# A hybrid decoder trunk on one core: evictions and gate additions issued with high priority

## The chip, the core and the metric

The kernel runs on one core of a Trainium2 chip. A core has a matrix engine (TensorE, PE in the profile, with its weight loads listed as PEld), three engines for element-wise work (VectorE or DVE, ScalarE or ACT, GpSimd or POOL) and SyncE (SP), which here only issues DMAs. Each engine has a queue of its own and works it off in order; engines wait for one another through semaphores. TensorE writes its results into PSUM, eight banks of 128 x 512 float32; another engine has to read a bank out ("evict" it) before it can be filled again.

The metric is device time in microseconds (us). The kernel before takes 806.76 us, the median of three runs (806.67 to 806.95).

## The reference, cut to what matters

Two residual layers over 256 tokens of width 1024. Each layer normalises the stream, multiplies it by one wide input matrix, feeds three causal mixers (a state-space scan, "SSD"; sliding-window attention with sinks, "SWA"; forgetting attention, "FOX"), projects each, weights the three by sigmoid gates with a bias, adds them, and applies an output projection:

```python
for layer in range(DEPTH):
    h = rms_norm(x, norm_w[layer])
    proj = jnp.einsum('bsd,de->bse', h, w_in[layer])
    (a_xbc, a_z, a_dt, b_q, b_k, b_v, b_z,
     c_q, c_k, c_v, c_f, c_z, gates) = jnp.split(proj, split_at, axis=-1)
    y_a = mamba2_branch(a_xbc, a_z, a_dt, ...)
    y_b = sliding_window_branch(b_q, b_k, b_v, b_z, ...)
    y_c = forgetting_attention_branch(c_q, c_k, c_v, c_f, c_z, ...)
    ys = jnp.stack([y_a, y_b, y_c], axis=2)
    branch = jnp.einsum('bsiw,iwd->bsid', ys, w_proj[layer])
    g = jax.nn.sigmoid(gates.reshape(b, s, N_BRANCH, d) + gate_bias[layer])
    merged = jnp.sum(g * branch, axis=2)
    x = x + jnp.einsum('bsd,de->bse', merged, w_out[layer])
return rms_norm(x, final_norm_w)
```

Everything is float32.

## The kernel before

**Products in three parts.** A float32 matrix is split into a high part, rounded to the format in which TensorE multiplies at full pace, and a low part, the remainder. A product is high x high + low x high + high x low. The splitting is work of its own: ScalarE copies the high part (line 290), VectorE subtracts it (line 291). Weights arrive as "raw" tiles of 128 x 1024 through SyncE's DMAs (line 360), six buffers deep, and are split into tiles `hi` and `lo`, six buffers each, up to four parts ahead of their use.

**Units.** The input matrix is worked off in units. A unit with *tokens on partitions* (`tok`) leaves a bank of 128 tokens x up to 512 columns. A unit with *channels on partitions* (`both_sums`) leaves 128 channels x 256 tokens, and it does so in one bank with two halves: the left half holds two of the three products, the right half the third. An eviction therefore has to add the halves, and there are two ways:

- `chan_sum` (lines 473 to 479): ScalarE copies the right half into the output (478), then VectorE adds the left half to it (479).
- `dma_sum` (lines 481 to 489): ScalarE copies both halves (486, 487), and a DMA issued by GpSimd adds one to the other in memory (488).

The keys, queries and gate paths of SWA, the convolution inputs of SSD and the first four key and query units of FOX use `dma_sum`; the gate paths of SSD and FOX and the other FOX units use `chan_sum`. Units write into three banks named `mm`; all other products (scores, transposes, scans) mostly use five banks named `mx`.

**Gates.** `u_gate` (line 1097 on) multiplies a 512-column unit of the gates, adds the bias from a tile that a DMA has spread over the partitions (VectorE, line 1106, or line 1108 in the first units, where the normalisation is still to be applied), and takes a tanh of half of it on ScalarE (1109). The merge (`merge`, from line 1134) multiplies the projected branch by the gate and adds it up; for the FOX branch it is issued with high priority. So are the output's operations in `out_end` (1205 on) and the sums of `u_proj_normed` (1017, 1019).

**What sets the order.** The order of TensorE's instructions is written out by hand: operations run in a fixed list, and the attention and scan steps are slipped in between by a small planner (`launch`, `pump`) that counts TensorE time and holds each step back for a fixed delay, so that its inputs are ready when TensorE comes to it. The other engines' order isn't written out after the first 13 us: a scheduler walks through the program and, whenever an engine is free in its model of time, takes the ready instruction with the lowest priority number. The number is the place in the program text, so earlier text goes first. Inside `with tc.high_priority():` it is that of the program's beginning, so such an instruction goes ahead of all other ready ones. On the chip the queues that come out of this are worked off strictly in order.

**Work hung behind evictions.** `finish(ins)` issues the deferred work of earlier units (convolution taps, rotations, gates' SiLU; list `ends_later`) and orders it behind the given instruction on that instruction's engine. `after_evictions(3, f)` puts f behind the third eviction from there, by when the accumulating DMA has landed.

**The window heads' softmax.** `attn_quad` handles four heads at once. For SWA, VectorE takes the row maxima (615, 623, 624), ScalarE the exponentials (610), VectorE the reciprocal sums and the product with them (638, 639); then TensorE transposes the probabilities (`mx<-ident,pp`, line 113).

Of the kernel before, what the change touches and what calls it, by code (L numbers as in the profile page):

```python
# [13 lines left out]
AF = mybir.ActivationFunctionType  # L14
ALU = mybir.AluOpType

P = 128
S = 256
# [32 lines left out]
def hybrid_trunk(  # L51
# [17 lines left out]
    def T(tag, shape, dtype=F32, bufs=None):  # L69
        count[0] += 1  # L70
        return sb.tile(shape, dtype, tag=tag, name=f"{tag}_{count[0]}",
                       bufs=bufs if bufs is not None else BUFS.get(tag, 1))
# [5 lines left out]
    def pmm():  # L78
        return PS("mm", 3)

    def pmx():
        return PS("mx", 5)

    act = nc.scalar.activation
    stt = nc.vector.scalar_tensor_tensor
    tt = nc.vector.tensor_tensor
# [63 lines left out]
    def pump(budget=BUDGET):  # L150
        t0 = clock["t"]
        half = False
        while True:
            over = clock["t"] - t0 >= budget
            if over and not half:
                return
            for m in sorted(waiting, key=lambda m: (m[5] and m[2] != 0, m[0], m[1])):
                if ready(m) and (m[5] if over else not early(m)):
                    half = m[5]
                    enter(m)  # L160
                    break
            else:
                return
# [112 lines left out]
    def ordered(ap):  # L276

        return ap.rearrange("p (i a) -> p a i", a=2)

    def halves(ap):  # L280

        return ap.rearrange("p (a i) -> p a i", a=2)
# [142 lines left out]
    for l in range(L):  # L425
        y = Layer()
# [46 lines left out]
    def chan_sum(y, w, c, out):  # L473


        p = pmm()
        both_sums(y, w, c, p)
        finish(act(halves(out), ordered(p[:, S:2 * S]), AF.Copy))
        tt(halves(out), ordered(p[:, 0:S]), halves(out), op=ALU.add)

    def dma_sum(y, w, c, out):

        p = pmm()
        both_sums(y, w, c, p)
        lo = T("L1", [P, S])
        act(halves(lo), ordered(p[:, S:2 * S]), AF.Copy)  # L486
        last = act(halves(out), ordered(p[:, 0:S]), AF.Copy)  # L487
        nc.gpsimd.dma_start(out, lo, accum_op=ALU.add)  # L488
        finish(last)

# [4 lines left out]
    def both_sums(y, w, c, p):  # L495
        for k in range(NK):
            if k > 0:
                mm(p[:, 0:S], w.lo(k)[:, c:c + P], tokens_in_turn(y.hTh, k), start=False, stop=False)
            mm(p, w.hi(k)[:, c:c + P], y.hT[:, k, :, :, :].rearrange("p a h i -> p (h i) a"),
               start=(k == 0), stop=(k == NK - 1))  # L500
            if k == 0:
                mm(p[:, 0:S], w.lo(k)[:, c:c + P], tokens_in_turn(y.hTh, k), start=False, stop=False)
            if w.last and (k + 1) % w.kper == 0:
                release(w, k // w.kper + 1)

    def tok(ah, al, w, t, turn=True, mid=None):


        n = w.n
        p = pmm()  # L510
        b = in_turn if turn else lambda ap: ap
        if mid is None and n > 300:
            mid = pump
        dense(p[:, 0:n], lambda k: ah[:, t, k, :], lambda k: al[:, t, k, :], lambda k: b(w.hi(k)),
              lambda k: b(w.lo(k)), w, mid=mid)
        return ordered(p[:, 0:n]) if turn else p[:, 0:n]
# [22 lines left out]
    def rotated(y, done):  # L539

        held = {}

        def u(half):
            def f(w):
                p = T("L1", [P, S])
                dma_sum(y, w, half * P, p)

                def turned():
                    for i in (half, 1 - half):
                        m = held[half, i] = T("L1", [P, S])  # L550
                        tt(m, p, cs[:, i, :], op=ALU.mult)  # L551
                    if half == 1:
                        done(held)
                after_evictions(3, turned)
                pump()
            return f
        return u(0), u(1)
# [256 lines left out]
    def u_conv(y, u, c):  # L814
        def f(w):
            if u == 8:
                y.bcT = T("L8", [P, 8, S])
            if u == 0:
                y.xs = T("L8", [P, 8, S])
            dst = y.xs[:, u, :] if u < 8 else y.bcT[:, u - 8, :]  # L820
            x_ = T("L1", [P, S])
            dma_sum(y, w, c, x_)

            def taps():
                a = T("L1", [P, S])
                act(a, x_, AF.Identity, scale=y.vec[:, 48 + u:49 + u], bias=y.vec[:, 64 + u:65 + u])  # L826
                for j in (2, 1, 0):
                    s = 3 - j
                    stt(a[:, s:S], x_[:, 0:S - s], y.vec[:, 16 * j + u:16 * j + u + 1], a[:, s:S],  # L829
                        op0=ALU.mult, op1=ALU.add)  # L830
                ends_later.append(lambda: end(a))

            def end(a):
                th = T("L1", [P, S])
                act(th, a, AF.Tanh)
                stt(dst, th, 1.0, a, op0=ALU.add, op1=ALU.mult)
                if u < 8 and u % 2 == 1:
                    launch(0, ssd_group(y, u // 2), D_G0)
            after_evictions(3, taps)
            pump()  # L840
        return f
# [4 lines left out]
    def finish(out):  # L846

        with tc.issue_after(out.ins):
            for _ in range(len(ends_later)):
                ends_later.pop(0)()  # L850
# [80 lines left out]
    def u_z(y, br, u, c):  # L931
        def f(w):
# [12 lines left out]
            if br == 1:  # L945
                dma_sum(y, w, c, o)
                after_evictions(3, gated)
                pump()
                return
            chan_sum(y, w, c, o)  # L950

            def normed():
# [92 lines left out]
    def u_ck(y, j, c):  # L1045
        def f(w):
            y.ckT[j] = T("qt", [P, 2, S])
            (dma_sum if j < EARLY else chan_sum)(y, w, c, y.ckT[j][:, 0, :])
            if j % 2 == 0:
                launch(2, fox_quad(y, j), D_FOX)  # L1050
            pump()
        return f

    def u_cq(y, j, c):
        def f(w):
            (dma_sum if j < EARLY else chan_sum)(y, w, c, y.ckT[j][:, 1, :])
            y.cqdone[j] = clock["t"] + (D_ADD if j < EARLY else 0.0)
            pump()
        return f
# [37 lines left out]
    def u_gate(y, br, c, t):  # L1097

        def f(w):
            if t == 0:  # L1100
                y.gb = T("L2", [P, 512])
                nc.scalar.dma_start(y.gb, gate_bias[y.l, br:br + 1, c:c + 512].to_broadcast([P, 512]))
            p = tok(y.hTh, y.hTl, w, t)
            g = T("L2", [P, 512])
            if y.rn is None:
                tt(halves(g), p, halves(y.gb), op=ALU.add)  # L1106
            else:
                stt(halves(g), p, y.rn[:, t:t + 1], halves(y.gb), op0=ALU.mult, op1=ALU.add)
            finish(act(g, g, AF.Tanh, scale=0.5))  # L1109
            y.gate[br, c, t] = g  # L1110
            pump()
        return f
# [312 lines left out]
    with tc.manual_schedule(engines={ENG.PE, ENG.DVE, ENG.Activation, ENG.Pool}):  # L1425
# [11 lines left out]
        p = pmx()  # L1437
# [93 lines left out]
        for i in range(2):  # L1531
# [6 lines left out]
                                op=ALU.add)  # L1538
# [53 lines left out]
```

## Time and profile before

| what | value |
|---|---|
| median of three runs | 806.76 us (806.67 to 806.95) |
| span of the profiled execution, first to last instruction | 805.1 us |
| what the median has beyond that span | 1.66 us |
| TensorE busy | 796.5 us (99%), mean granted clock 0.998 |
| VectorE busy | 684.2 us (85%) |
| ScalarE busy | 533.8 us (66%) |
| GpSimd busy | 167.5 us (21%) |

The profiled execution's own time outside of the profiler is not recorded separately; its span of 805.1 us is what the durations add up to, and 1.66 us lie around it in the median run.

How to read the lines: a group's line gives source line, engine, operation, output<-inputs by their tile tags (`L` stands for the general tiles L1, L2, L4, L8 and L16, `mm` and `mx` for the banks), shapes, the count, then busy time and mean ns, then the idle time of the engine just before these instructions and what ended it. A timeline line gives start, duration, engine, line, operation and count. A stretch's line gives start:end, its length, then the busy time of TensorE, weight loads, VectorE, ScalarE and GpSimd, the granted clock, the DMA share and GB/s. Matmuls overlap: one is recorded as longer than the distance to the next.

### The profile page before, as it was taken

How to read it: one execution, taken by the hardware profiler on the slowest of the kernel's cores; microseconds unless marked ns; L12 is line 12 of the kernel's file. 1: busy time of each engine (PE TensorE's matmuls, PEld its weight loads, DVE VectorE, ACT ScalarE, POOL GpSimd, SP SyncE). 2: the span in 40 equal slices, each digit the busy share in tenths (PEclk: the TensorE clock that was granted, in tenths of full speed). 3: DMA queues.
4: the chain of work that ended last, by engine and by line, in shares of the span. 5: the costliest groups of instructions: out<-in, count | busy, mean ns of one | idle time of the engine just before them, and what ended most of it. 6: DMA issues, size and time to landing. Idle time of an engine off the chain costs nothing.

```text
span 805.1 us, 14840 instructions
## 1 busy us (share of the span) xinstructions
PE 796.5 (99%) x5160; PEld 711.6 (88%) x5160; DVE 684.2 (85%) x1416; ACT 533.8 (66%) x1146; POOL 167.5 (21%) x236
## 2 busy tenths in 40 slices
PE   9999999999999999999999999999999999999996
PEld 8998988888998988888998899888889989888896
DVE  6878999997998997795785799999889999969865
ACT  7776768875775885543665678687657768755452
POOL 3166213140210100033001741122311220002000
PEclk9999999999999999999999999999999999999999
DMA  9997987797765565686678987679976546576632
GB/s 316 280 259 172 253 219 200 219 290 220 198 184 167 174 187 170 219 253 205 217 251 257 239 210 217 157 217 287 285 211 196 183 143 202 156 248 210 209 106 78
DMA packets 138827, 170.43 MB, mean 212 GB/s; under 512 B 9353, under 2 KB 106465, under 8 KB 138753
## 3 DMA queue, kind: packets, MB, share of 16 engines
q1 hardware_dynamic: 114960, 140.53, 55.5%
q0 software_dynamic: 13328, 13.29, 10.3%
q10 hardware_dynamic: 10464, 15.67, 6.7%
q8 instruction: 41, 0.67, 0.3%
q14 instruction: 34, 0.27, 0.1%
HBM read 154.71 MB, written 2.16 MB: 195 GB/s over the span
## 4 chain that ended last, share of the span: by engine, by line
PE 91%; issue 3%; DMA 2%; POOL 2%; DVE 1%; ACT 1%; POOLq 0%; DVEq 0%
PE mm L109 78%; PE mx L109 9%; PE mx L113 4%; DMA L<-L 1%; DMA hb<-in_sinks_dram 1%; POOL L L488 1%; DMA L<-in_x_dram 0%; DVE L L551 0%; ACT pp L610 0%; POOL L L285 0%; POOL L L562 0%; DVE lo L291 0%; POOL sm L224 0%; POOL L L571 0%; POOL L L572 0%
## 5 line engine op out<-in xcount | busy, mean ns | idle before, releaser
L109 PE MATMUL mm<-L,hi 128*128 128x512 f32 x1056 | 354.7, 387 | 0.5 <-ACT L L487 0.3
L291 DVE TENSOR_TENSOR lo<-raw,hi 128x1024 fp32r<-128x1024 f32 (+1 forms) x276 | 313.3, 1154 | 40.9 <-ACT hi L290 36.1
L109 PE MATMUL mm<-hi,L 128*128 128x512 f32 (+2 forms) x1168 | 303.1, 349 | 0.1
L290 ACT ACTIVATE hi<-raw 128x1024 fp32r<-128x1024 f32 (+1 forms) x276 | 265.6, 982 | 50.6 <-PE mm L109 30.0
L109 PE MATMUL mm<-L,lo 128*128 128x256 f32 x1056 | 266.6, 273 | 0.0
L109 PEld LDWEIGHTS mm<-hi,L 128*128 128x128 f32 x1168 | 205.8, 190 | 23.2 <-issue 1.5
L109 PEld LDWEIGHTS mm<-L,hi 128*128 128x128 f32 x1056 | 195.1, 190 | 27.4 <-issue 3.0
L109 PEld LDWEIGHTS mm<-L,lo 128*128 128x128 f32 x1056 | 202.1, 191 | 5.3
L109 PE MATMUL mm<-lo,L 128*128 128x512 f32 (+2 forms) x584 | 201.5, 347 | 0.0
L109 PEld LDWEIGHTS mm<-lo,L 128*128 128x128 f32 x584 | 110.2, 190 | 10.7
L488 POOL DMA_DIRECT2D L<-L x68 | 60.7, 915 | 192.5 <-ACT L L487 155.2
L1074 POOL TENSOR_SCALAR_AFFINE_SELECT bias<-bias 128x128 f32<-128x128 f32 x64 | 30.8, 513 | 82.7 <-DMA bias<-cumd 82.7
L829 DVE SCALAR_TENSOR_TENSOR L<-L,vec,L 128x255 f32<-128x255 f32 (+2 forms) x96 | 46.2, 481 | 1.9 <-ACT L L826 0.4
L486 ACT ACTIVATE L<-mm 128x256 f32<-128x256 f32 x84 | 31.9, 380 | 20.0 <-PE mm L109 14.0
L652 ACT ACTIVATE pp<-pp,nm 128x128 f32<-128x128 f32 x64 | 28.2, 443 | 22.8 <-DVE nm L646 22.8
L1109 ACT ACTIVATE L<-L 128x512 f32<-128x512 f32 x24 | 15.1, 631 | 34.5 <-DVE L L1106 30.8
L610 ACT ACTIVATE pp<-pp,nm 128x128 f32<-128x128 f32 x32 | 12.6, 394 | 24.9 <-DVE nm L615 24.1
L488 POOL DMA_DIRECT2D qt<-L x16 | 14.2, 925 | 71.4 <-ACT qt L487 64.6
L1142 POOL TENSOR_TENSOR L<-L,L 128x512 f32<-128x512 f32 x8 | 12.0, 1494 | 74.0 <-DVE L L1141 74.0
L487 ACT ACTIVATE L<-mm 128x256 f32<-128x256 f32 x68 | 26.2, 386 | 1.5 <-DMA L<-L 1.5
L1106 DVE TENSOR_TENSOR L<-mm,L 128x512 f32<-128x512 f32 x22 | 15.1, 687 | 11.2 <-PE mm L109 11.2
L551 DVE TENSOR_TENSOR L<-L,cs 128x256 f32<-128x256 f32 x40 | 20.0, 536 | 4.6 <-DMA L<-L 4.6
(213 smaller groups left out, 913.7 us busy)
## 6 DMA issues: line engine op xcount, KB each, us to landing
raw<-in_w_in_dram SPq DMA_DIRECT2D x191, 512.0 KB, 5.1
raw<-in_w_proj_dram SPq DMA_DIRECT2D x48, 512.0 KB, 6.0
L<-L POOLq DMA_DIRECT2D x72, 128.0 KB, 5.4
raw<-in_w_out_dram SPq DMA_DIRECT2D x16, 512.0 KB, 5.9
bias<-cumd ACTq DMA_DIRECT2D x16, 256.0 KB, 3.4
L<-cumd ACTq DMA_DIRECT2D x8, 512.0 KB, 5.4
L<-in_gate_bias_dram ACTq DMA_DIRECT2D x12, 256.0 KB, 5.4
qt<-L POOLq DMA_DIRECT2D x16, 128.0 KB, 6.0
```

The source lines that it names most:

```text
L109: nc.tensor.matmul(o, a, b, **kw)
L113: nc.tensor.transpose(o, a, i)
L290: keep(act)(hi, src, AF.Copy)
L291: keep(tt)(lo, src, hi.bitcast(F32), op=ALU.subtract)
L486: act(halves(lo), ordered(p[:, S:2 * S]), AF.Copy)
L487: last = act(halves(out), ordered(p[:, 0:S]), AF.Copy)
L488: nc.gpsimd.dma_start(out, lo, accum_op=ALU.add)
L551: tt(m, p, cs[:, i, :], op=ALU.mult)
L652: act(pp[:, i, sl], pp[:, i, sl], AF.Exp, scale=-1.0, bias=nm[:, e:e + 1], accum_out=sums[:, e:e + 1])
L829: stt(a[:, s:S], x_[:, 0:S - s], y.vec[:, 16 * j + u:16 * j + u + 1], a[:, s:S], op0=ALU.mult, op1=ALU.add)
L1074: nc.gpsimd.affine_select(out=bias[:, i, dst], in_=bias[:, i, src], compare_op=ALU.is_ge, fill=NEG, base=0, pattern=[[-1, P]], channel_mul ...
L1106: tt(halves(g), p, halves(y.gb), op=ALU.add)
```

## The change

In three places, reads of a bank are wrapped in `tc.high_priority()`: both steps of `chan_sum`, both copies of `dma_sum`, and the addition of the gates' bias in `u_gate`. In `chan_sum` the call of `finish` moves behind the addition, so deferred work that was written between the copy and the addition is now written behind both; it is still ordered behind the copy. The accumulating DMA of `dma_sum` and the gates' tanh keep their priority. No instruction is added or taken away.

```diff
         p = pmm()
         both_sums(y, w, c, p)
-        finish(act(halves(out), ordered(p[:, S:2 * S]), AF.Copy))
-        tt(halves(out), ordered(p[:, 0:S]), halves(out), op=ALU.add)
+        with tc.high_priority():
+            half = act(halves(out), ordered(p[:, S:2 * S]), AF.Copy)
+            tt(halves(out), ordered(p[:, 0:S]), halves(out), op=ALU.add)
+        finish(half)
 
     def dma_sum(y, w, c, out):
 
         p = pmm()
         both_sums(y, w, c, p)
         lo = T("L1", [P, S])
-        act(halves(lo), ordered(p[:, S:2 * S]), AF.Copy)
-        last = act(halves(out), ordered(p[:, 0:S]), AF.Copy)
+        with tc.high_priority():
+            act(halves(lo), ordered(p[:, S:2 * S]), AF.Copy)
+            last = act(halves(out), ordered(p[:, 0:S]), AF.Copy)
         nc.gpsimd.dma_start(out, lo, accum_op=ALU.add)
         finish(last)
...
             p = tok(y.hTh, y.hTl, w, t)
             g = T("L2", [P, 512])
-            if y.rn is None:
-                tt(halves(g), p, halves(y.gb), op=ALU.add)
-            else:
-                stt(halves(g), p, y.rn[:, t:t + 1], halves(y.gb), op0=ALU.mult, op1=ALU.add)
+            with tc.high_priority():
+                if y.rn is None:
+                    tt(halves(g), p, halves(y.gb), op=ALU.add)
+                else:
+                    stt(halves(g), p, y.rn[:, t:t + 1], halves(y.gb), op0=ALU.mult, op1=ALU.add)
             finish(act(g, g, AF.Tanh, scale=0.5))
```

## The prediction, made before the result was known

> **What bounds the kernel now.** I read the engines' busy time on the page first, then the sums by stretch, then the chain that ended last, then TensorE's own waits, and last the evictions. The page of the profile:
>
> ```profile
> span 805.1 us, 14840 instructions
> PE 796.5 (99%) x5160; PEld 711.6 (88%) x5160; DVE 684.2 (85%) x1416; ACT 533.8 (66%) x1146; POOL 167.5 (21%) x236
> ...
> PE 91%; issue 3%; DMA 2%; POOL 2%; DVE 1%; ACT 1%; POOLq 0%; DVEq 0%
> ```
>
> TensorE (PE) is busy 99% of the span, and the chain that ended last is PE for 91% of it. The sums by stretch (columns: PE, weight loads, VectorE, ScalarE, GpSimd) say where the other engines come close:
>
> ```profile
> 13.00:780.00 767.00, 766.44 (x4976) 684.24 (x4974) 660.54 (x1366) 516.34 (x1113) 165.15 (x221) 1.00 0.74 215
> 80.00:165.00 85.00, 84.83 (x634) 75.62 (x633) 81.23 (x200) 64.22 (x167) 19.97 (x26) 1.00 0.83 226
> 200.00:300.00 100.00, 100.00 (x743) 89.37 (x742) 94.23 (x252) 74.18 (x181) 14.20 (x28) 1.00 0.64 186
> 594.00:694.00 100.00, 100.00 (x744) 89.42 (x743) 93.94 (x251) 74.70 (x181) 14.38 (x28) 1.00 0.65 192
> ```
>
> From 13 to 780 us PE idles 0.56 us of 767. A busy PE could still be a slow PE, so the pace is taken from the chain (start, us, what, count):
>
> ```profile
> 3.59 4.01 PE mx L113 x18
> ...
> 349.88 10.36 PE mm L109 x48
> ...
> 401.34 0.87 PE mx L113 x8
> ```
>
> 48 matmuls of 512 columns in 10.36 us are 216 ns each. Transposes take 109 ns each in the middle (0.87 / 8) and 223 ns at the start (4.01 / 18), so the start alone runs at half pace. PE's own list of waits holds one wait on an eviction:
>
> ```profile
> PE mm L109 <- ACT L L487: 0.3, 1, 0.3
> ```
>
> That list understates: a matmul is recorded as 0.38 us long and the next begins 0.216 us after it, so a wait under 0.17 us isn't seen. Starts show more:
>
> ```profile
> 74.49 0.38 PE L109 MATMUL mm<-L,hi 128*128 128x512 f32 x1
> 75.19 0.48 PE L109 MATMUL mm<-L,hi 128*128 128x512 f32 x1 [0.31 <-ACT L L487]
> ...
> 123.63 0.38 PE L109 MATMUL mm<-L,hi 128*128 128x512 f32 x1
> 124.05 0.63 PE L113 MATMUL mx<-ident,pp 128*128 128x128 f32 x4
> 124.43 0.46 PE L109 MATMUL mm<-L,hi 128*128 128x512 f32 x1
> ...
> 150.04 0.69 DVE L1106 TENSOR_TENSOR L<-mm,L 128x512 f32<-128x512 f32 x1
> ...
> 150.36 0.97 PE L109 MATMUL mm<-L,hi 128*128 128x512 f32 x2
> ...
> 518.54 0.38 PE L109 MATMUL mm<-L,hi 128*128 128x512 f32 x1
> 518.96 0.52 PE L113 MATMUL mx<-ident,pp 128*128 128x128 f32 x3
> ...
> 545.27 0.87 PE L109 MATMUL mm<-L,hi 128*128 128x512 f32 x2
> ```
>
> 75.19 comes 0.70 after 74.49 instead of 0.22: 0.48 lost. At 124.05 and 518.96 the transposes of the softmax (pp) come 0.42 after the matmul: 0.20 lost each. The pair at 150.36 spans 0.97 where a pair with a 0.46 tail spans 0.68 (0.22 + 0.46): 0.3 lost; the pair at 545.27 in the same way 0.2. Together 1.4 us, of which bank waits on evictions are 0.48 + 0.3 + 0.2 = 1.0. So in the middle an ideal order of the other engines would gain 1.4 us, 0.17%.
>
> By the Trainium skill ("Trainium Kernel Development and Optimization", Best Practices, point 5) matmul busy time is a bad measure of the distance to the roofline and the weight loads' share is a good one; by it, with 88%, some 12% or 93 us would be open. The chain's 216 ns for 512 columns stands against that: weight loads can't fill 100% while each is followed by a longer stream.
>
> **The change part by part.** Which instructions move, by group (count, busy, mean ns | idle of the engine just before):
>
> ```profile
> L488 POOL DMA_DIRECT2D L<-L x68 | 60.7, 915 | 192.5 <-ACT L L487 155.2 <-ACT L L835 29.9 <-ACT L L942 4.5
> L486 ACT ACTIVATE L<-mm 128x256 f32<-128x256 f32 x84 | 31.9, 380 | 20.0 <-PE mm L109 14.0 <-DMA L<-L 3.1 <-POOL qt L561 1.0
> L487 ACT ACTIVATE L<-mm 128x256 f32<-128x256 f32 x68 | 26.2, 386 | 1.5 <-DMA L<-L 1.5
> L1106 DVE TENSOR_TENSOR L<-mm,L 128x512 f32<-128x512 f32 x22 | 15.1, 687 | 11.2 <-PE mm L109 11.2
> L488 POOL DMA_DIRECT2D qt<-L x16 | 14.2, 925 | 71.4 <-ACT qt L487 64.6 <-ACT L L835 6.8
> L479 DVE TENSOR_TENSOR L<-mm,L 128x256 f32<-128x256 f32 x32 | 13.3, 416 | 0.1
> L478 ACT ACTIVATE L<-mm 128x256 f32<-128x256 f32 x32 | 11.7, 365 | 0.0
> L479 DVE TENSOR_TENSOR qt<-mm,qt 128x256 f32<-128x256 f32 x16 | 6.7, 418 | 0.0
> ```
>
> No instruction is added or removed, and PE's order is written out by hand, so no duration changes: 84 units evicted in two steps by ScalarE (L486, L487), 48 by a ScalarE copy and a VectorE addition (L478, L479), 24 gate additions (22 as L1106, two in the form of L1108). What changes is what stands behind them in the queues of ScalarE and VectorE.
>
> *Gain: banks come free sooner.* Three eviction waits of PE, 1.0 us, can vanish; below nothing there is no room, above it 1.0. I take all of it, since each ended with an eviction of the groups above: at 75.19 L487 by the trace's own word, at 150.36 the gate's addition that ended at 150.73, with 545.27 as its twin in the second layer.
>
> *Cost: the softmax of the window heads.* ScalarE's pair takes 0.67 us (123.44 to 124.11):
>
> ```profile
> 123.21 0.69 DVE L639 TENSOR_TENSOR pp<-pp,rsum 128x512 f32<-128x512 f32 x1
> ...
> 123.44 0.39 ACT L486 ACTIVATE L<-mm 128x256 f32<-128x256 f32 x1
> 123.71 0.40 ACT L487 ACTIVATE L<-mm 128x256 f32<-128x256 f32 x1
> ```
>
> Here the pair stands behind the quad's exponentials, which L639 needs; L639 ends at 123.90 and PE's transposes of 124.05 wait for it. If the pair is put ahead, the exponentials and L639 come 0.67 later, and so does PE: twice (one per layer), 1.3 us. Bounds: 0, if the order stays, and 0.67 for each of the 8 quads (four per layer), 5.4 us. I take 1.3: only these two products are seen to hold PE up.
>
> *The VectorE additions.* A prioritised addition stands at the head of its queue and, where its producer is late, VectorE idles. The trace has that price for operations that have the priority already, and for one without it:
>
> ```profile
> L1019 DVE SCALAR_TENSOR_TENSOR L<-mx,rs,L 128x512 f32<-128x512 f32 x16 | 11.9, 745 | 1.4 <-PE mx L109 1.1
> L1145 DVE SCALAR_TENSOR_TENSOR L<-L,mm 128x512 f32<-128x512 f32 x6 | 4.1, 682 | 5.2 <-PE mm L109 5.2
> ```
>
> L479 now idles 0.1 / 48 = 0.00 us each, L1019 1.4 / 16 = 0.09, L1145 5.2 / 6 = 0.87. I take 0.09, the row nearest in kind: it too adds bank after bank of a running sum. 24 additions per layer then cost 2.2 us of VectorE in a stage where it has 100 - 94.23 = 5.77 us free (6.06 in the second layer): hidden, 0. The gates at 0.69 each move ahead of weight splits; they cost 0 as long as the splits keep their lead, and PE's waits hold none on a split.
>
> *Queues.* The 84 accumulating DMAs on GpSimd (L488, 0.92 each) follow their pair and start sooner; their queue waits 192.5 + 71.4 us for ScalarE today: 0. SyncE's loads wait for the low halves of the splits,
>
> ```profile
> SPq L360 <- DVE lo L291: 409.1, 173, 13.5
> ```
>
> so a split that is passed by an addition (0.42 or 0.69) delays its load by as much, with six raw buffers ahead: 0. In the first 13 us the order of all engines is written by hand, and after 780 only operations run that have the priority already or aren't touched: 0.
>
> *Sum.* -1.0 + 1.3 + 0 = +0.3. The profiled execution spans 805.1 us; 806.76, the median of three runs, lies 1.66 us above that span, and I leave these 1.66 as they are: 805.1 + 1.66 + 0.3 = 807.1 us. A change of 0.2% is 1.6 us, about what a measurement of this kernel can tell from none; the forecast is no change.
>
> **The rivals.**
>
> *Nothing moves.* Where VectorE is late, ScalarE waits for it and the evictions behind wait too, whatever their priority:
>
> ```profile
> ACT pp L610 <- DVE nm L615: 24.1, 8, 6.5
> ```
>
> Eight waits, the longest 6.5 us. If the exponentials were placed by time and not by priority, the order stays and so does the time: 806.8. It ends on the forecast's side.
>
> *VectorE held by its additions (slower).* Place: the stages 200 to 300 and 594 to 694, where VectorE fills 94 of 100 us. An addition at the head waits for its ScalarE copy, which waits behind exponentials that wait for VectorE. Price: 24 times the idle time per addition, less 5.77 and 6.06. It decides from 5.77 / 24 = 0.24 us each; at 0.30 it is 7.2 - 5.77 + 7.2 - 6.06 = 2.6, so 807.1 + 2.6 = 809.7; at 0.35 it is 5.0, so 812. For it: 0.87 at L1145. Against: 0.09 at L1019.
>
> *The softmax late in most quads (slower).* Five of the eight quads at 0.67 are 3.4, less the gain of 1.0: 809.2. It decides from four. For it: 81.23 of 85 us on VectorE there. Against: only the two places shown have no lead.
>
> *A wait that slows PE's clock (slower).* At the start PE runs at half pace, 223 against 109 ns per transpose, for at least the 4.0 us of that row. If one wait as long as the longest loss seen, 0.48, brought this back for as long, it would cost 0.48 and half of 4.0: 807.1 + 2.5 = 809.6. Against: after the wait at 75.19 matmuls go on at full pace (the 0.38 us rows). The Trainium skill ("TensorE: Matmul & The Clock Gate", What's actually happening) has the array fall to half its clock after an idle window of about 3.4 us; by that the price is an estimated 5.1 us, and no wait of this trace is long enough.
>
> *PE is not at its floor (faster).* The first matmul behind the transposes is recorded as 0.46, not 0.38 (124.43). If that 0.08 were a wait for a bank that sooner evictions end, 156 units would gain 12.5: 794.3. Against: it begins 0.38 after the first of four transposes, which take 0.436 at 109 ns, so it only began early.
>
> **How the numbers follow.** Forecast 0.40, nothing moves 0.15, VectorE held 0.23, softmax late 0.14, slow clock 0.03, PE not at its floor 0.05. Faster by over 0.2%: 0.05; within: 0.55; slower: 0.23 + 0.14 + 0.03 = 0.40. The forecast's own range is 805.4 (all 1.4 gained) to 808.1 (1.0 more lost). The range of 8 in 10 reaches from 805.5 up to 812.0, VectorE held at 0.35.
>
> **What would show it.** Right: PE's idle time from 13 to 780 stays near 0.56, the wait on L487 at 75.19 is gone, idle before L479 stays under 0.24 per addition, and pp's transposes come some 0.7 later at 124 and 519. Wrong: PE waits on low halves (L291) or on L479 in 200 to 300, or idle before L479 above 5.8 us per layer; or a span under 803.5.

## The result

The changed kernel takes 809.1 us, the median of eight runs (808.7 to 809.76); the kernel before took 806.91 us in as many runs beside it (806.67 to 807.96). The ratio is 1.0026, with a 95% interval of 1.0016 to 1.0036: slower by 2.2 us, where the forecast was 807.1 and no change. The line numbers of the changed kernel are shifted: the pair of copies is 489 and 490 (486 and 487 before), the addition of `chan_sum` 480, the gate's addition 1110, the exponentials 613, the small exponentials 638 (635), the sums 639 (636), the normalisation of the probabilities 642 (639), the taps 832 (829).

### The profile after

The page of the changed kernel, the lines that answer to those of before:

```profile
span 807.7 us, 14831 instructions
PE 797.5 (99%) x5160; PEld 712.6 (88%) x5160; DVE 686.0 (85%) x1416; ACT 533.8 (66%) x1146; POOL 169.9 (21%) x236
...
PE 90%; DVE 6%; ACT 1%; issue 1%; DMA 0%; ACTq 0%
```

The span of the profiled execution grew by 2.6 us, from 805.1 to 807.7. TensorE has the same 5160 instructions, in the same order, and 1.0 us more busy time. What is new is in the chain that ended last: 6% of it now runs through VectorE, where it was 1%. The sums by stretch (PE, weight loads, VectorE, ScalarE, GpSimd) say where:

```profile
13.00:780.00 767.00, 765.16 (x4959) 682.75 (x4958) 660.83 (x1365) 515.46 (x1113) 167.51 (x221) 1.00 0.75 215
80.00:165.00 85.00, 84.18 (x630) 74.86 (x629) 80.66 (x199) 64.30 (x167) 18.84 (x25) 1.00 0.81 218
200.00:300.00 100.00, 100.00 (x744) 89.45 (x744) 93.37 (x248) 73.84 (x180) 15.79 (x28) 1.00 0.64 184
```

From 13 to 780 us TensorE now idles 767.00 - 765.16 = 1.84 us, where it was 0.56. It idles nothing from 200 to 300, where VectorE's moved additions are closest together; 0.82 us of it lies from 80 to 165 (0.17 before). TensorE's own list of waits, after:

```profile
PE mm L109 <- DVE L L1110: 0.9, 2, 0.6
PE mx L113 <- ACT pp L613: 0.5, 2, 0.3
...
PE mx L113 <- DVE pp L642: 0.2, 1, 0.2
```

The wait on an eviction by ScalarE (0.3 on L487) is gone. Two waits on the gate's addition (L1110) and three on the softmax of the window heads (pp) have come. The starts show their size, by the prediction's own way of reading them: the first row of each two is TensorE's instruction before the wait.

```profile
99.83 0.28 PE L109 MATMUL mm<-lo,L 128*128 128x272 f32 x1
100.35 0.63 PE L113 MATMUL mx<-ident,pp 128*128 128x128 f32 x4 [0.24 <-DVE pp L642]
...
124.52 0.38 PE L109 MATMUL mm<-L,hi 128*128 128x512 f32 x1
125.16 0.63 PE L113 MATMUL mx<-ident,pp 128*128 128x128 f32 x4 [0.25 <-ACT pp L613]
...
151.46 0.38 PE L109 MATMUL mm<-L,hi 128*128 128x512 f32 x1
152.17 0.45 PE L109 MATMUL mm<-L,hi 128*128 128x512 f32 x1 [0.33 <-DVE L L1110]
...
495.74 0.28 PE L109 MATMUL mm<-lo,L 128*128 128x272 f32 x1
496.14 0.63 PE L113 MATMUL mx<-ident,pp 128*128 128x128 f32 x4
...
520.31 0.38 PE L109 MATMUL mm<-L,hi 128*128 128x512 f32 x1
520.95 0.63 PE L113 MATMUL mx<-ident,pp 128*128 128x128 f32 x4 [0.26 <-ACT pp L613]
...
547.26 0.38 PE L109 MATMUL mm<-L,hi 128*128 128x512 f32 x1
548.26 0.45 PE L109 MATMUL mm<-L,hi 128*128 128x512 f32 x1 [0.62 <-DVE L L1110]
```

The first place before had no wait at all:

```profile
99.37 0.28 PE L109 MATMUL mm<-lo,L 128*128 128x272 f32 x1
99.49 0.60 PE L113 MATMUL mx<-ident,pp 128*128 128x128 f32 x4
```

Gap by gap, after less before: 0.52 - 0.12 = 0.40 at 100; 0.64 - 0.42 = 0.22 at 125; 0.71 - 0.51 = 0.20 at 152; 0.40 - 0.12 = 0.28 at 496; 0.64 - 0.42 = 0.22 at 521; 1.00 - 0.41 = 0.59 at 548. (150.87 and 545.68 are the starts of the second matmuls of the pairs that the prediction showed at 150.36 and 545.27; the gap of 0.12 at 494.40 is that of 99.49.) The six places make 1.9 of the 2.6 us. Most of the rest is the start of the program: TensorE was 1.04 us later at 10 us, and 0.58 of that went again at 75, where the kernel before waited. The last 0.16 came at 305 us.

### What comes ahead of those six places

The softmax of the second window quad on ScalarE, before:

```profile
97.07 0.35 ACT L610 ACTIVATE pp<-mx,nm 128x128 f32<-128x128 f32 x1
...
97.42 0.35 ACT L610 ACTIVATE pp<-mx,nm 128x128 f32<-128x128 f32 x1
...
97.76 0.29 ACT L635 ACTIVATE es<-es 128x4 f32<-128x4 f32 x2
97.95 0.36 ACT L486 ACTIVATE L<-mm 128x256 f32<-128x256 f32 x1
```

and after:

```profile
97.64 0.37 ACT L489 ACTIVATE L<-mm 128x256 f32<-128x256 f32 x1
97.90 0.38 ACT L490 ACTIVATE L<-mm 128x256 f32<-128x256 f32 x1
98.17 0.37 ACT L613 ACTIVATE pp<-mx,nm 128x128 f32<-128x128 f32 x1
...
98.51 0.38 ACT L613 ACTIVATE pp<-mx,nm 128x128 f32<-128x128 f32 x1
...
98.85 0.31 ACT L638 ACTIVATE es<-es 128x4 f32<-128x4 f32 x2
```

The pair of copies of the convolution's unit 11 stood behind two exponentials and two small exponentials; now it stands ahead of them. Only three `dma_sum` pairs per layer overtake anything in the stage of the window heads: this one, that of a gate path (`z1`, u = 1 of the second branch, at 75 us), which passes one small exponential, and that of the convolution's unit 14 (at 124 us), which passes one exponential and one small exponential. VectorE takes the small exponentials into its sums, and what follows in VectorE's queue stands behind. The group of these sums (count, busy, mean ns | idle time of VectorE just before them), before:

```profile
L636 DVE TENSOR_TENSOR sums<-sums,es 128x4 f32<-128x4 f32 x16 | 2.4, 161 | 0.8 <-ACT es L635 0.4
```

and after:

```profile
L639 DVE TENSOR_TENSOR sums<-sums,es 128x4 f32<-128x4 f32 x16 | 2.3, 163 | 3.1 <-ACT es L638 2.8
```

Single sums of that group in the timeline after, those that waited (in square brackets the idle time before them):

```profile
75.94 0.26 DVE L639 TENSOR_TENSOR sums<-sums,es 128x4 f32<-128x4 f32 x2 [0.22 <-ACT es L638]
...
99.11 0.25 DVE L639 TENSOR_TENSOR sums<-sums,es 128x4 f32<-128x4 f32 x2 [0.73 <-ACT es L638]
...
125.25 0.17 DVE L639 TENSOR_TENSOR sums<-sums,es 128x4 f32<-128x4 f32 x1 [0.24 <-ACT es L638]
...
541.28 0.16 DVE L639 TENSOR_TENSOR sums<-sums,es 128x4 f32<-128x4 f32 x1 [0.38 <-ACT es L638]
```

VectorE waits 3.1 us there instead of 0.8. The 2.3 us more are about as much as the kernel lost (2.2). That is a reading, not yet a proof; the experiments test it.

### The profile page after: what moved, and what is told of

It reads as the page before. It is cut to its first block, busy times and chain, and to the rows that moved or that the text cites. A ratio compares the mean times of both kernels' runs of the same rounds, so it can differ in the third digit from the quotient of the medians.

```text
span 807.7 us, 14831 instructions
## 1 busy us (share of the span) xinstructions
PE 797.5 (99%) x5160; PEld 712.6 (88%) x5160; DVE 686.0 (85%) x1416; ACT 533.8 (66%) x1146; POOL 169.9 (21%) x236
## 4 chain that ended last, share of the span: by engine, by line
PE 90%; DVE 6%; ACT 1%; issue 1%; DMA 0%; ACTq 0%
PE mm L109 78%; PE mx L109 8%; PE mx L113 4%; DVE lo L291 2%; DVE L L832 1%; ACT pp L613 1%; DMA L<-in_x_dram 0%; DVE pp L618 0%; DVE L L784 0%; ACT hi L290 0%; DVE mx L626 0%; DVE pp L642 0%; DVE L L1110 0%; DVE L L726 0%; DVE L L679 0%
## 5 line engine op out<-in xcount | busy, mean ns | idle before, releaser
L1077 POOL TENSOR_SCALAR_AFFINE_SELECT bias<-bias 128x128 f32<-128x128 f32 x64 | 32.8, 545 | 86.0 <-DMA bias<-cumd 49.5
L838 ACT ACTIVATE L<-L 128x256 f32<-128x256 f32 x32 | 13.4, 419 | 17.2 <-DVE L L832 17.2
L988 POOL TENSOR_TENSOR sm<-sm,mhalf 128x8 f32<-128x8 f32 x2 | 3.4, 1686 | 96.7 <-DVE sm L986 96.7
```

What stands on the lines that cost most here:

```text
L1077: nc.gpsimd.affine_select(out=bias[:, i, dst], in_=bias[:, i, src], compare_op=ALU.is_ge, fill=NEG, base=0, pattern=[[-1, P]], channel_mul ...
```

## The experiments

**Theory A**: a pair of copies put ahead of small exponentials makes VectorE wait at the sums. VectorE has next to no idle time of its own in this stage, so it stays late, and TensorE pays wherever it next takes something from VectorE: at the probabilities (100, 125 us) and at the bank that the gate's addition frees (152 us). The other moves of the change do nothing. The rivals are written in the expectations. Medians below are of 4 to 11 runs each; the kernel before, beside them, took 807.07, 807.05, 806.97 and 806.96 us in the four groups of runs.

### Only the three pairs, and all but the three pairs

The kernel before with the priority for these three pairs per layer alone (`dma_sum` takes a flag; the second place is `u_conv`, the third the gate path of SWA):

```
-    def dma_sum(y, w, c, out):
+    def dma_sum(y, w, c, out, high):
...
+        with tc.high_priority() if high else ExitStack():
...
-            dma_sum(y, w, c, x_)
+            dma_sum(y, w, c, x_, u in (11, 14))
...
-                dma_sum(y, w, c, o)
+                dma_sum(y, w, c, o, u == 1)
```

> The kernel before, with priority for three of the 42 two-copy evictions of each layer only: the gate path's second unit and the convolution's units 11 and 14. Theory A (these pairs stand between a quad's exponentials in ScalarE's queue, VectorE idles for it and PE waits later): the whole loss, 806.9 + 2.2 = 809.1 us, and PE's waits at about 99, 124 and 151 us grow as in the changed kernel. Rival B (the additions on VectorE in the stages 200 to 300 and 594 to 694): 806.9. Rival C (the start, which was 1.0 us later in the changed kernel's profile, is part of the change): 806.9 + 1.2 = 808.1 or less.

Measured: 809.1 us (808.47 to 810.04), ratio 1.0025 (1.0015 to 1.0034). The whole loss is there.

The changed kernel without the priority for these pairs, and with it for all other `dma_sum` and `chan_sum` units and all gate additions (the lines are those of the changed kernel):

```
-        with tc.high_priority():
+        with tc.high_priority() if high else ExitStack():
...
-            dma_sum(y, w, c, x_)
+            dma_sum(y, w, c, x_, u not in (11, 14))
...
-                dma_sum(y, w, c, o)
+                dma_sum(y, w, c, o, u != 1)
```

> The changed kernel, without priority for the three pairs per layer: all additions and the other 39 pairs keep it. Theory A: 806.9 us, no difference from the kernel before (interval holds 1). Rival B: 809.1. Rival C: 807.9 or more.

Measured: 807.06 us (806.57 to 807.76), ratio 1.0 (0.9991 to 1.0009). The sums by VectorE, in the first and in the second of these kernels:

```profile
L637 DVE TENSOR_TENSOR sums<-sums,es 128x4 f32<-128x4 f32 x16 | 2.3, 164 | 3.1 <-ACT es L636 2.7
```

```profile
L639 DVE TENSOR_TENSOR sums<-sums,es 128x4 f32<-128x4 f32 x16 | 2.4, 160 | 0.8 <-ACT es L638 0.4
```

3.1 us of idle time with the loss, 0.8 without. Six pairs of copies carry all of it; the additions of VectorE, the gates, the DMAs of GpSimd and the other 78 pairs carry nothing that the medians show, in either direction. (By TensorE's starts they cost 0.15 us, once, at 305 us: 0.13 to 0.16 in the four profiles that move the additions, 0.01 at most in the others.) The gate's additions at 152 and 548 us have no priority in the first of the two kernels, and TensorE waits for them all the same: the gate at 152 us isn't late because it was moved, but because VectorE is.

### One of the pairs, and a second profile of the change

The flag for the convolution's unit 11 alone (`u == 11`):

> The kernel before, with priority for one pair per layer, that of the convolution's unit 11, which passes two exponentials and two small exponentials. Theory A: VectorE's later work moves by 0.68 us per layer, as in the changed kernel (its lag in the second layer rises from 1.31 to 2.00 there), and PE's end by the same: 806.9 + 1.36 = 808.3. If VectorE makes it up before PE needs it: 806.9.

Measured: 808.01 us (807.7 to 808.25), ratio 1.0011 (1.0002 to 1.002). Of the three pairs' 2.0 us (809.1 - 807.07) this one makes 0.9, less than the 1.4 expected. The trace shows the path that Theory A asks for. Against the same operations in the profile before, VectorE runs 0.13 us later up to 97.7 us, 0.67 later from the sums on, where it waited 0.72 us for the small exponentials, and still 0.69 at the gate's addition of 150 us. TensorE runs 0.14 us later up to 99 us, 0.44 behind the transposes of 100 us and 0.66 behind those of 125. So the loss at 125 us comes from a wait of VectorE's 25 us earlier, and once TensorE is as late as VectorE it loses nothing more: at the gates' banks this run has no loss of its own.

The flag for the gate path's pair alone (`u == 1` in the gate path of SWA):

> The kernel before with priority for one pair of copies per layer: that of the second u_z unit of the first branch, whose unit ends at 69.6 us. In the order it overtakes only one small exponential of a sum. Theory A (a pair that overtakes a softmax makes VectorE wait for ScalarE, and VectorE, which has no idle time of its own from 65 to 151 us, hands the lost time to TensorE at the next place where TensorE takes something from it): one small exponential is one pair of copies late, at most 0.3 us per layer, 0.6 in all: 807.0 to 807.6. Rival D (the loss comes only from an exponential of a whole row block put behind a pair): nothing is lost, 806.9.

Measured: 806.79 us (806.59 to 807.51), ratio 1.0 (0.9991 to 1.0009). VectorE waits 0.22 us per layer more for a small exponential at 75 us, and nothing is lost. That is below the 807.0 to 807.6 that Theory A asked for and is what rival D foretold. The reading that fits the traces is that VectorE idles behind that place in any case: from 80 to 95 us it is busy 14.25 of 15 us in this run and 13.88 in the run with unit 11's pair, so 0.75 us are left of 1.12. From 95 to 125 us it is busy 29.30 of 30, with 0.7 us in twice the time. By this reading the price of a wait of VectorE's depends on the idle time that lies between it and the next thing that TensorE takes; a small exponential alone, put behind a pair where VectorE is full, was not run.

Unit 14's pair didn't run alone. If the three prices simply added up, it would have 2.0 - 0.9 - 0 = 1.1 us. By the traces it has the loss at the gates' banks, 0.19 at 152 us and 0.56 at 548 in the profile of the three pairs: VectorE is 0.94 us late there up to the probabilities' product of 124 us, 1.25 from the sum behind unit 14's pair on and 1.13 at the gate, where TensorE goes from 0.94 to 1.13.

The changed kernel as it is, profiled again:

> The changed kernel once more, for a second profile. If the 1.0 us later start of its first profile is chance: the start lies within 0.3 us of that of the kernel before (first weight product at 7.3 us), and the time is 809.1 all the same, since the loss is in the middle. If it belongs to the change: again 1.0 us.

Measured: 808.81 us (808.2 to 809.71), ratio 1.0024 (1.0015 to 1.0033). TensorE's lag behind the kernel before grows at the same six places (0.29, 0.22, 0.19, 0.27, 0.22, 0.56). The late start (1.04 us in the first profile) is 0.54 here, still above the 0.3 expected. It isn't the change's all the same: the profile before has the earliest start of all fourteen, and kernels whose order is untouched up to 74 us are late by as much (0.71 with unit 11's pair, 0.68 before with two taps).

### More of ScalarE's time ahead of the same exponentials

Two more copies of the same bank, into the same tile, with the same priority as unit 11's pair:

```
         with tc.high_priority() if high else ExitStack():
+            for _ in range(2 if high else 0):
+                act(halves(lo), ordered(p[:, S:2 * S]), AF.Copy)
             act(halves(lo), ordered(p[:, S:2 * S]), AF.Copy)
```

> The kernel with priority for the pair of the convolution's unit 11 alone, and two more copies of the bank's second half ahead of that pair (they write the same tile, the output is the same): ScalarE's work ahead of the overtaken exponentials goes from 0.67 to about 1.2 us. Theory A: what VectorE waits for ScalarE grows by the added 0.5 us at each of the two places, and TensorE with it: from 808.0 of the single pair to 808.8 to 809.2. Rival C (the order itself, or where things fall in memory, not ScalarE's time): no more than the single pair, 808.0.

Measured: 808.68 us (808.4 to 809.47), ratio 1.0026 (1.0015 to 1.0036). The first sum of the second quad, with the pair alone and with four copies:

```profile
98.66 0.26 DVE L637 TENSOR_TENSOR sums<-sums,es 128x4 f32<-128x4 f32 x2 [0.72 <-ACT es L636]
```

```profile
99.09 0.26 DVE L639 TENSOR_TENSOR sums<-sums,es 128x4 f32<-128x4 f32 x2 [1.26 <-ACT es L638]
```

VectorE waits 0.54 us longer per layer, 1.08 in both, and the median rises by 0.67, somewhat less than the 0.8 to 1.2 expected. TensorE is 0.01 us behind the kernel before at 75 us, 0.85 at 100 and 0.94 at 125; with the pair alone it is 0.14, 0.41 and 0.66. It loses more at the first place, by about what VectorE waited more, and hardly anything at the second. What it has waited at the one place it need not wait at the next; that is the likely reason, but VectorE's order also differs from 105 us on (two weight splits and a tap change places), and no run separates the two.

ScalarE's order isn't quite that of the kernel with one pair: the added copies stand one ahead of each of the last two exponentials, and the pair behind these, ahead of the small exponentials alone. Up to 105 us VectorE's order is the same in both. Rival C allowed 808.0 at most, and the loss at 100 us grew where nothing but ScalarE's queue differs: what grew is ScalarE's work ahead of the small exponentials that VectorE waits for.

### VectorE with slack

The kernel before with the convolution's tap j = 0 left out, 32 VectorE operations of 0.48 us, so that its output is that of a shorter convolution; then the three pairs on that kernel; then the whole change on it:

```
-                for j in (2, 1, 0):
+                for j in (2, 1):
```

> The kernel before with the convolution's tap j = 0 left out (32 VectorE operations of some 0.48 us; the output is that of a convolution that is one tap shorter). Theory A: VectorE has slack now; TensorE's waits for VectorE at 124, 150, 519 and 545 us, 0.9 us in sum, go away: about 806.0. Rival: TensorE waits there for something that is not VectorE's load: 806.9.

> The three pairs per layer with priority, and the same tap of the convolution left out. Theory A: with slack on VectorE the time that it waits for ScalarE is made up before TensorE asks for anything: at most 0.5 us above the kernel before without the tap. Rival D (the late softmax stops TensorE directly, and only what is handed on to the gates' banks at 152 and 548 us is VectorE's): 1.5 us above it (0.73 + 0.24 + 0.28 + 0.25 of the run of the three pairs). Rival E (VectorE's load plays no part): 2.2 us above it, as with all taps.

> The whole change on the kernel without the convolution's tap j = 0 (the output is that of a convolution that is one tap shorter). Theory A (the whole price of the change is time of VectorE's): as the kernel before without the tap, 805.6 to 806.2. Rival G (other parts of the change cost TensorE something of their own): 806.5 or more.

Measured, in this order: 805.86 us (805.27 to 806.3), ratio 0.9988 (0.998 to 0.9997); 805.74 (805.45 to 806.35), ratio 0.9986 (0.9977 to 0.9995); 805.94 (805.54 to 806.57), ratio 0.9989 (0.998 to 0.9997); each ratio is to the kernel before with all taps. With slack on VectorE the loss is gone. VectorE's wait is not gone. (Leaving out the taps also moves a few operations on VectorE and ScalarE; the pairs pass the same exponentials as with all taps.) The sums in the second of these kernels, and its stretch from 13 to 780 us:

```profile
L637 DVE TENSOR_TENSOR sums<-sums,es 128x4 f32<-128x4 f32 x16 | 2.3, 164 | 2.9 <-ACT es L636 2.5
```

```profile
13.00:780.00 767.00, 766.99 (x4987) 685.92 (x4987) 649.51 (x1337) 518.22 (x1116) 168.50 (x221) 1.00 0.76 216
```

VectorE idles 2.9 us ahead of the sums, as with all taps, and TensorE idles 0.01 us. So the delayed exponentials stop TensorE only by way of a VectorE that can't catch up. Rival D, in which the late softmax stops TensorE directly, asked for 1.5 us above the first of the three kernels, and rival E, in which VectorE's load plays no part, for 2.2; measured is -0.1. The first of the three runs also settles what the waits of the kernel before are worth: without VectorE's lateness TensorE idles nothing, and the time falls by 807.05 - 805.86 = 1.2 us.

All runs that tell the theories apart, in one table (idle time of VectorE ahead of the sums; idle time of TensorE from 13 to 780 us, each from the profiled execution):

| kernel | VectorE ahead of the sums | TensorE idle | median, us |
|---|---|---|---|
| before | 0.8 | 0.56 | 806.76 to 807.07 |
| all but the three pairs | 0.8 | 0.30 | 807.06 |
| gate path's pair | 1.2 | 0.38 | 806.79 |
| unit 11's pair | 1.9 | 0.96 | 808.01 |
| unit 11's, four copies | 2.9 | 1.60 | 808.68 |
| three pairs | 3.1 | 2.12 | 809.1 |
| the change | 3.1 | 1.84 | 809.1 |
| the change, second profile | 3.0 | 1.66 | 808.81 |
| before, two taps | 0.9 | 0.00 | 805.86 |
| three pairs, two taps | 2.9 | 0.01 | 805.74 |
| the change, two taps | 2.8 | 0.00 | 805.94 |

### Can VectorE be relieved without leaving work out?

GpSimd is busy 21%. One tap of the convolution moved to it would give VectorE the slack:

```
+                    if j == 2 and u >= 8:
+                        m = T("L1", [P, S])
+                        nc.gpsimd.tensor_scalar(m, x_, y.vec[:, 16 * j + u:16 * j + u + 1], None, op0=ALU.mult)
+                        gtt(a[:, s:S], m[:, 0:S - s], a[:, s:S], op=ALU.add)
+                        continue
                     stt(a[:, s:S], x_[:, 0:S - s], y.vec[:, 16 * j + u:16 * j + u + 1], a[:, s:S],
```

> The kernel before, with the first of the convolution's three taps done on GpSimd (a multiplication and an addition into the same tile) for units 8 to 15; the output is the reference's. Theory A (VectorE's load between 65 and 151 us sets the last waits of TensorE): eight operations of 0.48 us fewer on VectorE per layer, the waits at 124, 150, 519 and 545 us go away: 805.8 to 806.3, faster than both kernels. Rival F (VectorE now waits for GpSimd, whose two operations take some 2 us by the rows of its 128x256 operations, or is slowed by it while both work): 807.5 or more.

The same with `u in (9, 11, 13, 15)`:

> As the run with eight units, for units 9, 11, 13 and 15 alone: 1.9 us of VectorE per layer. Theory A: TensorE waits for VectorE for 0.2 to 0.5 us per layer, so half the relief does: 805.8 to 806.4. Rival F: 807.2 or more.

Measured: 820.47 us (818.91 to 822.18), ratio 1.0162 (1.0148 to 1.0176), and 817.86 (815.88 to 818.34), ratio 1.0129 (1.0115 to 1.0143). That is rival F (807.5 or more, and 807.2 or more). GpSimd's two groups in the kernel with eight units (count, busy, mean ns | idle before), then a line of VectorE's waits and one of TensorE's (us in total, times, longest):

```profile
L831 POOL TENSOR_SCALAR L<-L,vec 128x256 f32<-128x256 f32 x16 | 23.9, 1493 | 5.5 <-DMA L<-L 5.5
L832 POOL TENSOR_TENSOR L<-L,L 128x255 f32<-128x255 f32 x16 | 14.0, 877 | 8.8 <-issue 4.5 <-ACT L L826 3.7
```

```profile
DVE L L834 <- POOL L L832: 13.5, 14, 1.8
```

```profile
PE mm L109 <- DVE L L1111: 4.0, 2, 2.0
```

GpSimd takes 1.49 us for the multiplication and 0.88 for the addition, where VectorE took 0.48 for the tap; VectorE waits 13.5 us for it, and TensorE waits 2.0 us at the gates' bank in each layer. The 16 x 0.48 = 7.7 us taken off VectorE are outweighed. The Trainium skill ("Perfetto Trace Analysis", Optimizing Scalar/DVE Operations) says that offloading a saturated VectorE may make sense, but that a move to GpSimd might not help, since the two share a read port; the trace agrees in the outcome (13.5 us slower), and no run here separates the port from the plain length of GpSimd's operations.

Not all of the loss is waiting. Behind that wait TensorE itself is slow; its row and the sums of two microseconds soon after, in the kernel with eight units:

```profile
156.88 0.45 PE L109 MATMUL mm<-L,hi 128*128 128x512 f32 x1 [1.99 <-DVE L L1111]
```

```profile
158.00:160.00 2.00, 2.00 (x8) 1.65 (x6) 1.39 (x4) 1.38 (x5) 0.87 (x1) 0.50 1.07 329
```

The granted clock is 0.50 there, for 3.4 us in all. In the three kernels of this section (the third comes below) TensorE waits 2.0 to 2.1 us at this bank six times; four of these waits are followed by 3.4 us at half the clock, and TensorE falls another 1.3 to 1.6 us back. No other profile has the clock below 1.00 from 13 to 780 us, and waits of up to 1.1 us didn't bring it on.

A last version issues the two taps left to VectorE one eviction later, so that GpSimd would have its time:

```
+                    after_evictions(1, lambda: more(a, (1, 0)))
```

> As the run with units 9, 11, 13 and 15 on GpSimd, but the two taps left to VectorE are issued one eviction later, some 1.9 us of TensorE's units behind GpSimd's addition (GpSimd's two operations took 1.39 and 0.64 us in that run). If VectorE's waits for GpSimd (10.5 us in that run, longest 2.0) were the whole of its loss, they go, and the relief of VectorE shows: 805.8 to 806.8. If the waits remain, because GpSimd is late itself or the order puts other work behind it, 810 to 818.

Measured: 816.7 us (815.31 to 817.79), ratio 1.0118 (1.0101 to 1.0135). VectorE still waits 12.4 us for GpSimd, eight times, at most 2.0, which is the second branch of the expectation. A version faster than the kernel before was not found; the 1.2 us that two taps showed are there, but not by way of GpSimd in these three forms.

## Why the prediction was right or wrong, point by point

The range from 805.5 to 812.0 us holds the time, and by luck: the forecast's own range ended at 808.1, and what carries the wide one up to 812.0 is VectorE held by its additions, which didn't happen. The forecast itself, no change and 807.1, was 2.0 us short, by two steps of its sum.

**What bounds the kernel.** Right. With VectorE relieved, in the kernel before with two taps, TensorE is busy 767.00 of 767.00 us, and 1.2 us is all that its waits were worth; the prediction had 1.4 from the trace. In that same stretch the weight loads make 686.81 us, 90%: no idle time is left, and the share of the weight loads is still not 100%. The 12% that the Trainium skill's rule on weight loads would leave open ("Trainium Kernel Development and Optimization", Best Practices, point 5) aren't there.

**The gain of 1.0 us: wrong, all of it.** The step said that three bank waits "can vanish". The wait at 75.19 belonged to one execution. In the kernel with all but the three pairs the pair of copies at that place has no priority, and the wait isn't there either. VectorE's wait for a transfer ahead of it, and TensorE's start, before and in that kernel:

```profile
65.41 0.76 DVE L551 TENSOR_TENSOR L<-L,cs 128x256 f32<-128x256 f32 x2 [3.22 <-DMA L<-L]
```

```profile
64.36 0.76 DVE L554 TENSOR_TENSOR L<-L,cs 128x256 f32<-128x256 f32 x2 [1.84 <-DMA L<-L]
...
74.83 0.60 PE L109 MATMUL mm<-L,hi 128*128 128x512 f32 x2
```

The transfer landed 1.05 us earlier there, in absolute time, and two matmuls in 0.60 us (0.22 + 0.38) have no wait between them. None of the other kernels' profiles has this wait in TensorE's list; by the starts, the one with four copies has 0.2 us of it. In the first profile of the change ScalarE's pair ran at nearly the same time as before (74.45 against 74.50), and the wait is gone because TensorE came 1.04 us later. The two waits on the gate's additions didn't vanish but grew, by 0.20 and 0.59: the additions stand between the same neighbours on VectorE as before, priority or not, and what ended the waits was VectorE's lateness, not its order.

**The cost of 1.3 us for the softmax: right in kind, but its place and its path misread.** The step took one quad per layer, at 0.67 us, since "only these two products are seen to hold PE up". At the place that was named, unit 14's pair can't hold up the transposes of 124.05. The product that these wait for, the L639 of 123.21, starts before the exponential that the pair passes has ended. In the rows of before, the first is the small exponential that this product needs. The pair passes the second and the third, which feed the sum of 123.82 and the second L639, at 124.23:

```profile
122.57 0.20 ACT L635 ACTIVATE es<-es 128x4 f32<-128x4 f32 x1
...
123.01 0.37 ACT L610 ACTIVATE pp<-mx,nm 128x128 f32<-128x128 f32 x1
...
123.35 0.21 ACT L635 ACTIVATE es<-es 128x4 f32<-128x4 f32 x1
...
123.82 0.16 DVE L636 TENSOR_TENSOR sums<-sums,es 128x4 f32<-128x4 f32 x1
```

What was lost at 125 and 521 us was 0.22 each and not 0.67, and it came from unit 11's pair: with that pair alone, and unit 14's without priority, the same 0.22 is lost there. Three of four quads per layer were overtaken, six of eight; of these the first costs nothing alone (806.79) and the second, which had no visible wait at all, costs 0.9 us (808.01 alone). What the step left out is that the lost time doesn't end at the probabilities. A product without a visible wait has little lead either when VectorE, which makes it, is full: the prediction quoted VectorE's 81.23 of 85 us as what speaks for more than one quad, and let "only the two places shown have no lead" outweigh it. Unit 14's pair was paid for behind the softmax, at the gates' banks, 0.79 us in sum.

**VectorE's additions at 0: right, to the 0.15 us at 305 us.** VectorE idles 0.3 us ahead of the 32 additions of the one form, 0.01 each, against the 0.09 that the step took, and TensorE idles nothing from 200 to 300 or from 594 to 694. **The gates and the queues at 0: right**, as all but the three pairs at 807.06 shows.

**The rivals.** "The softmax late in most quads" said 809.2 and had a chance of 0.14; it comes closest to what happened, 809.1, with six quads overtaken where it counted five, a smaller price for each, and a path through VectorE that it didn't name. That its number is so close is partly luck: it subtracted the gain of 1.0, which wasn't there. "VectorE held by its additions" said 809.7, near in number too, and its mechanism isn't there. The clock didn't fall after the longest wait, 0.78 us at 548.26: the rows behind it start at 548.77 and 549.10, 0.33 apart with a matmul of half the columns between, as before the wait. That rival was right that a wait can do it, at a longer one: waits of 2.0 us were followed by half the clock four times in six in the kernels with taps on GpSimd, without the idle window of 3.4 us that the prediction quotes, at 1.3 to 1.6 us each. And the forecast itself: -1.0 should have been 0, +1.3 should have been 2.2.

**The signs it named.** Two of its four signs of being right came: the wait at 75.19 is gone, if for another reason, and the idle time ahead of the additions is 0.01 us. Two didn't: TensorE's idle time rose from 0.56 to 1.84, and the transposes of 124 and 519 us came 0.22 later than TensorE already was, not 0.7. None of its signs of being wrong came.

**What stays open.** The loss at 100 us was 0.73 us with the three pairs alone and 0.40 and 0.29 in the two profiles of the change, with the same order on ScalarE and VectorE there. The traces say where the difference lies: at 95 us VectorE was later than TensorE (each against the profile before) by 0.44, 0.11 and 0.00 us, and 0.29 with these added gives the three losses. What makes VectorE more or less late by then stays open; the landing of the transfer at 65 us and the gate path's pair both come before it, and no run here takes them apart. Open too is why two of the six waits of 2.0 us weren't followed by half the clock.

## What to carry to other kernels

A wait that one profiled execution shows is a sample: before it is entered as a gain, ask what it hung on, and if that is a transfer's landing or the start of the program, enter it as nothing. For a reordering, list every place where the moved work passes something that another engine takes, not only those where the bottleneck is seen to wait: where the engine in between has next to no idle time, its wait is handed on to the next place where the bottleneck takes something from it, however far from the move. And what an engine waits for can be small: VectorE stood still for a 128x4 exponential of 0.2 us, the last of a row of work that had been put behind 0.67 us of copies.

## What the runs showed of the hardware that was not expected

A wait of TensorE's of 2.0 us was followed by 3.4 us at half the granted clock in four cases of six, which cost 1.3 to 1.6 us beyond the wait; waits of up to 1.1 us weren't.

At 10 us the other thirteen profiles are 0.34 to 1.14 us behind that of the kernel before, though the order of work in the first 13 us, written out by hand, is the same, and part of a late start costs nothing, where TensorE would otherwise have waited (0.58 us at 75 us). Of the 1.04 us in the first profile of the change, 0.7 came between 7.5 and 8.9 us, where neighbouring matmuls of 256 columns still start some 0.2 us apart; those of the profile before start 0.11 apart there.

GpSimd took 0.88 us for a 128x255 addition with eight units on it and 0.64 us with four, so the recorded length of one operation differs by 40%; one profile shows 1.25 us for one of them while VectorE was splitting weights for most of that time. No run shows what sets it.
